# First loads on the sync engine's queue, and the first norm's statistics half a step later in a SwiGLU gate and up loop

## The chip, the cores and the metric

The kernel runs on one core of a Trainium2 chip. The core has five engines that run side by side, each through its own list of instructions in order: TensorE (PE in the profile; its weight loads are PEld), VectorE (DVE), ScalarE (ACT), GpSimd (POOL) and SyncE (SP). Data comes from HBM into SBUF by DMA; SP, ACT and POOL issue the transfers, and a transfer lands some microseconds after its issue. Products are summed in PSUM banks, of which the kernel keeps six in a pool called `sd` and two in a pool called `mm`.

The metric is the device time of one execution in microseconds. Before the change it is 1267.71 us, the median of three runs from 1267.32 to 1268.02.

## The reference, cut to what matters

Two layers, each of a SwiGLU block, a mixer (attention and gated linear attention) and another SwiGLU block, on 256 tokens of width 1024. The change touches only the very first SwiGLU block:

```python
def rmsnorm(x, g):
    xf = x.astype(jnp.float32)
    y = xf * lax.rsqrt(jnp.mean(xf * xf, axis=-1, keepdims=True) + EPS)
    return (y * g.astype(jnp.float32)).astype(x.dtype)

def swiglu(x, w_gate, w_up, w_down):
    return (jax.nn.silu(x @ w_gate) * (x @ w_up)) @ w_down

x = x + 0.5 * swiglu(rmsnorm(x, ffn1_norm[l]), ffn1_w_gate[l], ffn1_w_up[l], ffn1_w_down[l])
```

## The kernel before

The tokens lie transposed: eight blocks of 128 features by 256 tokens (`self.x`, tile `xs`). Every float32 operand is split into a high part in a reduced format and a low part, the rest: `split_x` (lines 158 to 164) multiplies a block by the norm's gain, makes the high part on ACT (L161) and the low part on DVE (L162). Weights come as chunks of up to 1 MB. `Weights.load` issues a chunk's transfer on SP into a tile `raw` (three of them), `cast` makes the high part `wh` of half a chunk on ACT (L76), and `prep` calls `cast` for the next half and then makes the low part `wl` of the half cast before it on DVE (L86). A product is two matmuls, `wh` against both parts of x (L129, 512 columns) and `wl` against the high part (L130, 256 columns).

`ffn` (line 237) runs 22 steps for gate and up. Chunk i holds the gate and the up weights of step i, each 128 columns wide: the first half of the chunk is the gate's, the second half is the up's. A step has 8 pairs of matmuls for the gate into one bank of `sd` (tile `ff`), and 8 for the up into a second. So step 3 cannot do its up before the second half of chunk 3 has its low part. The norm's factor for a token does not go into x: the matmuls run on x times the gain, and the results are multiplied by the factor (`rbc`) afterwards. Until `rbc` is there, finished banks wait.

For a finished step, `gate` adds the two halves of the gate's bank (a copy on ACT, L138, and an add on DVE, L139), multiplies by `rbc` (L248) and takes the Silu on ACT (L249); `gate2` multiplies by `rbc` (L253); `up` does L138 and L139 on the up's bank, multiplies the two (L260) and makes the high part on ACT (L261). The low part of the result (L265) is put off in the list `lows`.

`rbc` comes from a chain: squares of x on ACT (L1153), three adds on DVE (L1182 to L1185) that leave `acc`, a sum over the partitions on PE (`stat`, tile `st`), mean and eps on DVE (`rstd_col`, L192), the power −0.5 on POOL (L194), a broadcast over the partitions on PE (`rstd_row`, tile `rb`, L150) and a copy (L202) on DVE. In the first block (`start`) step 0 mixes gate and up and only waits; `stat` stands on PE after the gate of step 1, `rstd_row` after its up; then the gate and up of steps 0 and 1 are finished together.

The order on every engine is the order in which the code issues (a manual schedule). At the start, `go` loads x in four quarters on ACT's queue and chunk 0 in four quarters on SP's, then chunk 1 in three pieces, part of the constants, and chunk 2 in two; a small Silu on ACT brings in its table (L1114), and PE multiplies zeros (`wb`, L150) until data is there.

Of the kernel before, what the change touches and what calls it, by code (L numbers as in the profile page):

```python
# [17 lines left out]
T = 256  # L18
# [83 lines left out]
class Trunk:  # L102
# [75 lines left out]
        self._uid = getattr(self, "_uid", 0) + 1  # L178
        return self._uid

    def stat(self):
        self.st = self.bank(f"st{self.uid()}")
        self.sums(self.acc, True, True)

    def sums(self, sq, first, last):
# [7 lines left out]
        self.rs = self.small([P, 2], "rs")  # L193
        nc.gpsimd.tensor_tensor(self.rs, ms, self.mhalf[:, 0:2], op=OP.pow)  # L194

    def rstd_row(self):
        nc = self.nc
        b = self.bank(f"rb{self.uid()}")
        for tt in range(2):
            self.mm(b[:, tt * P : tt * P + P], self.rs[:, tt : tt + 1].to_broadcast([P, P]), self.ident)  # L200
        self.rbc = self.prb.tile([P, T], F32, name=f"rbc{self.uid()}", tag="rbc")
        nc.vector.tensor_copy(self.rbc, b[:, 0:T])  # L202
# [34 lines left out]
    def ffn(self, l, f, next_gain, hook=None):  # L237
        nc, W = self.nc, self.W
        start = l == 0 and f == 0
        hs = []  # L240
        lows = []

        def gate(i, b):

            u = self.t2(f"u{self.uid()}")
            g = u[:, 0:T]
            self.halves(g, b)
            nc.vector.tensor_mul(g, g, self.rbc)  # L248
            nc.scalar.activation(g, g, AF.Silu)  # L249
            return u  # L250

        def gate2(u):
            nc.vector.tensor_mul(u[:, 0:T], u[:, 0:T], self.rbc)  # L253

        def up(i, u, b):
            if i % 2 == 0:
                hs.extend(self.splits("h", 2))
            h = u[:, T : 2 * T]
            self.halves(h, b)
            nc.vector.tensor_mul(h, u[:, 0:T], h)  # L260
            nc.scalar.activation(hs[i][0], h, AF.Copy)  # L261
            lows.append((hs[i][1], h, hs[i][0].bitcast(F32)))

        def low():
            nc.vector.tensor_sub(*lows.pop(0))  # L265

        wait = None
        for i in range(NFF):
            wh, wl = W.take()
            bs = [self.bank(f"ff{self.uid()}") for _ in range(2)]  # L270
            if i == 0:
                for k in range(NK):
                    for n in range(2):
                        r = n * NK + k
                        self.mm2(bs[n], wh[:, r], wl[:, r], self.xx[k], k == 0, k == NK - 1)
                if not start:
                    self.stat()
                    self.rstd_col()
                    W.prep()
                W.prep()  # L280
                wait = bs
                continue
            for k in range(NK):
                self.mm2(bs[0], wh[:, k], wl[:, k], self.xx[k], k == 0, k == NK - 1)
            if i == 1:
                if start:
                    self.stat()
                    self.rstd_col()
                    self.constants()
                else:  # L290
                    self.rstd_row()
                    u0 = gate(0, wait[0])
                    gate2(u0)
                    up(0, u0, wait[1])
            if not (i == 1 and start):
                u = gate(i, bs[0])
            W.prep()
            if not (i == 1 and start):
                gate2(u)
            for k in range(NK):  # L300
                self.mm2(bs[1], wh[:, NK + k], wl[:, NK + k], self.xx[k], k == 0, k == NK - 1)
            if i == 1 and start:
                self.rstd_row()
                u0 = gate(0, wait[0])
                W.prep()
                gate2(u0)
                up(0, u0, wait[1])
                u = gate(i, bs[0])
                W.prep()
                gate2(u)  # L310
                up(i, u, bs[1])
            else:
                up(i, u, bs[1])
                W.prep()
            low()
            if hook:
                hook(i)
        while lows:
            low()
        for j in range(NK):  # L320
            b = self.bank(f"dn{self.uid()}", "mm")
            for half in range(2):
                wh, wl = W.take()
                for r in range(11):
                    k = half * 11 + r
                    self.mmx(j, b, wh[:, r], wl[:, r], hs[k], k == 0, k == NFF - 1)
                if half == 0 or j < NK - 1:
                    W.prep()
                    W.prep()
                if next_gain is None and half == 0 and j > 0:  # L330
                    self.final_x(j - 1)
                    if j == NK - 1:
                        self.st = self.bank("stl")
                        self.sums(self.acc, True, False)
            self.add_half(j, b)
            if next_gain is None:
                self.square(j, own=j == NK - 1)
                xg = self.t2(f"xg{j}")[:, 0:T]
                nc.vector.tensor_scalar(xg, self.x[j], self.final[:, j : j + 1], None, op0=OP.mult)
                self.xg[j] = xg  # L340
            else:
                self.post_x(j, next_gain[:, j : j + 1])
        W.prep()
        W.prep()
# [717 lines left out]
    def go(self):  # L1062
        from contextlib import ExitStack

        nc, tc, a = self.nc, self.tc, self.a
        with ExitStack() as st:
# [35 lines left out]
            sm = cp.tile([P, 80], F32, name="sm")  # L1102
            first = pools["raw"].tile([P, 2048], F32, name="raw0", tag="raw")
            view = lambda t, p: t.rearrange("p (n k c) -> p n k c", n=2, k=NK)[:, :, 2 * p : 2 * p + 2, :]

            for p in range(4):
                nc.scalar.dma_start(self.xs[:, 2 * p : 2 * p + 2, :], a["x"][:, 2 * p : 2 * p + 2, :])
                nc.sync.dma_start(view(first, p), view(a["gu"][0, 0, 0], p))
                if p == 0:
                    nc.scalar.dma_start(sm, a["sm"])  # L1110
            W.n_load = 1
            warm = self.small([P, 2], "warm", 1)
            nc.vector.memset(warm, 0.0)
            nc.scalar.activation(warm, warm, AF.Silu)  # L1114

            idle = self.t2("idle")
            nc.vector.memset(idle, 0.0)
            wb = self.bank("wb")
            for n in range(7):
                self.mm(wb[:, n % 2 * T : n % 2 * T + T], idle[:, 0:P], idle[:, 0:T])  # L1120
            gain = lambda l, n: sm[:, (l * 3 + n) * 8 : (l * 3 + n) * 8 + 8]
            self.final = sm[:, 48:56]
# [15 lines left out]
            nc.vector.memset(self.mhalf, -0.5)  # L1138
            w0 = W.split[0] = tuple(pools["w"].tile([P, 2048], F32R, name=f"w{x}0", tag=f"w{x}") for x in "hl")
            for p in range(4):  # L1140
                for j in (2 * p, 2 * p + 1):
                    self.split_x(j, gain(0, 0)[:, j : j + 1])
                nc.scalar.activation(view(w0[0], p), view(first, p), AF.Copy)  # L1143
                nc.vector.tensor_sub(view(w0[1], p), view(first, p), view(w0[0], p).bitcast(F32))  # L1144
            w1 = W.split[1] = tuple(pools["w"].tile([P, 2048], F32R, name=f"w{x}1", tag=f"w{x}") for x in "hl")
            for s in (slice(0, 512), slice(512, 1024)):
                nc.scalar.activation(w1[0][:, s], W.raw[1][:, s], AF.Copy)
                nc.vector.tensor_sub(w1[1][:, s], W.raw[1][:, s], w1[0][:, s].bitcast(F32))
            W.at, W.n_prep = (1, 1), (1, 0)
            W.load(1 + N_RAW)  # L1150
            sq = [self.t4(f"sq{x}") for x in range(2)]
            for x in range(2):
                nc.scalar.activation(sq[x].rearrange("p (j t) -> p j t", j=4), self.xs[:, 4 * x : 4 * x + 4, :], AF.Square)  # L1153
# [24 lines left out]
                    nc.gpsimd.memset(t, 0.0)  # L1178

            self.constants = constants  # L1180
            W.cast()
            nc.vector.tensor_add(sq[0], sq[0], sq[1])  # L1182
            nc.vector.tensor_add(sq[0][:, 0:512], sq[0][:, 0:512], sq[0][:, 512:1024])
            self.acc = self.psq.tile([P, T], F32, name="acc0", tag="acc")
            nc.vector.tensor_add(self.acc, sq[0][:, 0:256], sq[0][:, 256:512])  # L1185
            W.prep()

            def bias_hook(i):
                if i == 5:
# [34 lines left out]
            for tt in range(2):  # L1224
                for e in range(2):
                    o = self.t2(f"out{tt}{e}")
                    b = self.fin[tt][e]
# [92 lines left out]
```

## Time and profile before

| | |
|---|---|
| median of three runs | 1267.71 us |
| profiled execution | 1268.17 us |
| its span | 1266.4 us |
| PE busy | 1251.6 us, 99% |
| DVE busy | 913.9 us, 72% |
| ACT busy | 711.8 us, 56% |

The span runs from the first to the last instruction in the trace; the profiled execution is 1.77 us longer than its span. Times in the rows are counted from the span's start. PE's ends are modelled, so starts are the safer number there. Where a row merges several instructions (x2, x3), it gives the first start and the time to the last end.

### The profile page before, as it was taken

How to read it: one execution, taken by the hardware profiler on the slowest of the kernel's cores; microseconds unless marked ns; L12 is line 12 of the kernel's file. 1: busy time of each engine (PE TensorE's matmuls, PEld its weight loads, DVE VectorE, ACT ScalarE, POOL GpSimd, SP SyncE). 2: the span in 40 equal slices, each digit the busy share in tenths (PEclk: the TensorE clock that was granted, in tenths of full speed). 3: DMA queues.
4: the chain of work that ended last, by engine and by line, in shares of the span. 5: the costliest groups of instructions: out<-in, count | busy, mean ns of one | idle time of the engine just before them, and what ended most of it. 6: DMA issues, size and time to landing. Idle time of an engine off the chain costs nothing.

```text
span 1266.4 us, 18985 instructions
## 1 busy us (share of the span) xinstructions
PE 1251.6 (99%) x7396; PEld 1076.0 (85%) x7396; DVE 913.9 (72%) x1690; ACT 711.8 (56%) x1265; POOL 50.5 (4%) x60
## 2 busy tenths in 40 slices
PE   9999999999999999999999999999999999999997
PEld 7888889987778888888888888999777788888886
DVE  6888766774755778886578886567656668888753
ACT  5666545566644556655456664456675445566542
POOL 2001101000010000000010000010000100000000
PEclk9999999999999999999999999999999999999999
DMA  7576767334534445545665546573344354555451
GB/s 272 193 230 211 255 201 264 132 124 137 178 118 144 181 168 205 187 154 198 209 224 208 179 150 205 173 283 135 111 156 164 103 199 148 184 200 185 165 190 59
DMA packets 41001, 227.43 MB, mean 180 GB/s; under 512 B 6949, under 2 KB 8109, under 8 KB 21328
## 3 DMA queue, kind: packets, MB, share of 16 engines
q1 hardware_dynamic: 34352, 213.27, 48.7%
q0 software_dynamic: 5840, 11.87, 2.8%
q8 instruction: 58, 0.95, 0.3%
q10 hardware_dynamic: 720, 1.09, 0.3%
q14 instruction: 31, 0.25, 0.1%
HBM read 225.12 MB, written 2.63 MB: 180 GB/s over the span
## 4 chain that ended last, share of the span: by engine, by line
PE 80%; issue 15%; DVE 2%; ACT 2%; DMA 1%; POOL 0%; POOLq 0%; DVEq 0%; ACTq 0%
PE ff L129 19%; PE ff L130 10%; PE dn L129 9%; PE mm L122 7%; PE mm L123 6%; PE mm L124 6%; PE dn L130 4%; PE wo L129 2%; PE mg L122 2%; PE mg L124 2%; PE mg L123 2%; PE O L150 2%; PE o L150 1%; PE s L150 1%; PE wo L130 1%
## 5 line engine op out<-in xcount | busy, mean ns | idle before, releaser
L76 ACT ACTIVATE wh<-raw 128x1024 fp32r<-128x1024 f32 (+3 forms) x445 | 423.4, 967 | 183.6 <-issue 112.3
L86 DVE TENSOR_TENSOR wl<-raw,wh 128x1024 fp32r<-128x1024 f32 (+3 forms) x445 | 491.3, 1119 | 44.0 <-ACT wh L76 43.7
L129 PE MATMUL ff<-xs,wh 128*128 128x512 f32 x1408 | 489.9, 392 | 0.4 <-DVE xs L162 0.4
L130 PE MATMUL ff<-xs,wl 128*128 128x256 f32 x1408 | 393.9, 280 | 0.7 <-DVE wl L1144 0.5
L129 PEld LDWEIGHTS ff<-xs,wh 128*128 128x128 f32 x1408 | 264.4, 188 | 59.2 <-ACT wh L1143 0.8
L130 PEld LDWEIGHTS ff<-xs,wl 128*128 128x128 f32 x1408 | 264.3, 188 | 1.7 <-DVE wl L1144 1.1
L129 PE MATMUL dn<-h,wh 128*128 128x512 f32 x616 | 218.3, 399 | 0.0
L130 PE MATMUL dn<-h,wl 128*128 128x256 f32 x616 | 173.0, 281 | 0.0
L129 PEld LDWEIGHTS dn<-h,wh 128*128 128x128 f32 x616 | 115.7, 188 | 28.3
L139 DVE TENSOR_TENSOR u<-ff,u 128x256 f32<-128x256 f32 x176 | 74.7, 425 | 60.9 <-ACT u L138 60.9
L130 PEld LDWEIGHTS dn<-h,wl 128*128 128x128 f32 x616 | 116.4, 189 | 0.0
L122 PE MATMUL mm<-wh,xs 128*128 128x512 f32 x256 | 106.2, 415 | 2.5 <-DVE rt L541 2.5
L123 PE MATMUL mm<-wl,xs 128*128 128x512 f32 x256 | 101.5, 396 | 0.0
L124 PE MATMUL mm<-wh,xs 128*128 128x512 f32 x256 | 100.9, 394 | 0.0
L249 ACT ACTIVATE u<-u 128x256 f32<-128x256 f32 x88 | 36.8, 419 | 90.8 <-DVE u L248 90.8
L261 ACT ACTIVATE h<-u 128x256 fp32r<-128x256 f32 x88 | 36.8, 418 | 83.9 <-DVE u L260 83.9
L122 PE MATMUL mm<-xs,wh 128*128 128x256 f32 x256 | 73.8, 288 | 0.0
L124 PE MATMUL mm<-xs,wl 128*128 128x256 f32 x256 | 71.7, 280 | 0.0
L123 PE MATMUL mm<-xs,wh 128*128 128x256 f32 x256 | 71.6, 280 | 0.0
L138 ACT ACTIVATE u<-ff 128x256 f32<-128x256 f32 x176 | 65.6, 373 | 9.8 <-PE ff L130 5.4
L355 DVE SCALAR_TENSOR_TENSOR xs<-dn,xs 128x256 f32<-128x256 f32 x60 | 25.5, 424 | 56.0 <-PE dn L130 38.5
L122 PEld LDWEIGHTS mm<-wh,xs 128*128 128x128 f32 x256 | 48.1, 188 | 19.3 <-issue 4.7
(244 smaller groups left out, 1618.1 us busy)
## 6 DMA issues: line engine op xcount, KB each, us to landing
raw<-in_gu SPq DMA_DIRECT2D x85, 1024.0 KB, 4.9
raw<-in_wd SPq DMA_DIRECT2D x64, 704.0 KB, 4.1
raw<-in_wr SPq DMA_DIRECT2D x32, 1024.0 KB, 4.8
raw<-in_wt SPq DMA_DIRECT2D x16, 1024.0 KB, 5.1
raw<-in_wb SPq DMA_DIRECT2D x12, 1024.0 KB, 4.8
w<-in_w POOLq DMA_DIRECT2D x16, 512.0 KB, 8.6
raw<-in_wo SPq DMA_DIRECT2D x8, 1024.0 KB, 4.9
raw<-in_vg SPq DMA_DIRECT2D x4, 592.0 KB, 3.7
```

Source lines behind the costliest of these rows:

```text
L76: self.nc.scalar.activation(wh[:, s], self.raw[c][:, s], AF.Copy)
L86: self.nc.vector.tensor_sub(wl[:, s], self.raw[c][:, s], wh[:, s].bitcast(F32))
L122: mm(out, lh, rh, start=first, stop=False, skip_group_check=True)
L123: mm(out, lh, rl, start=False, stop=False, skip_group_check=True)
L124: mm(out, ll, rh, start=False, stop=last, skip_group_check=True)
L129: mm(b, lh, x[2], start=first, stop=False, skip_group_check=True)
L130: mm(b[:, 0:T], ll, x[0], start=False, stop=last, skip_group_check=True)
L138: self.nc.scalar.activation(o, b[:, T : 2 * T], AF.Copy)
L139: self.nc.vector.tensor_add(o, b[:, 0:T], o)
L150: self.nc.tensor.matmul(out, l, r, start=first, stop=last, skip_group_check=True)
L249: nc.scalar.activation(g, g, AF.Silu)
L261: nc.scalar.activation(hs[i][0], h, AF.Copy)
```

## The change

First loads: ACT issues only the first quarter of x and the small table of gains; SP issues the rest, quarters of x and of chunk 0 in turn. PE multiplies zeros five times in place of seven, on a tile cleared to half its width. In the first splits, a quarter of chunk 0 is cast between the two blocks of x that go with it.

Statistics: the second half of chunk 1 and the first half of chunk 2 are cast on ACT before the squares, and the low part of chunk 1's second half is made before the adds of the squares. `stat` moves behind the up of step 1, `rstd_row` behind the gate of step 2; both take their bank from the pool `mm`. Steps 0 and 1 are then finished after `rstd_row`, in the middle of step 2, one after the other with no `prep` between. The loops for the other three SwiGLU blocks come out in the order they had.

```diff
-    def stat(self):
-        self.st = self.bank(f"st{self.uid()}")
+    def stat(self, tag="sd"):
+        self.st = self.bank(f"st{self.uid()}", tag)
...
-    def rstd_row(self):
+    def rstd_row(self, tag="sd"):
         nc = self.nc
-        b = self.bank(f"rb{self.uid()}")
+        b = self.bank(f"rb{self.uid()}", tag)
...
             for k in range(NK):
                 self.mm2(bs[0], wh[:, k], wl[:, k], self.xx[k], k == 0, k == NK - 1)
-            if i == 1:
-                if start:
-                    self.stat()
-                    self.rstd_col()
-                    self.constants()
-                else:
-                    self.rstd_row()
-                    u0 = gate(0, wait[0])
-                    gate2(u0)
-                    up(0, u0, wait[1])
-            if not (i == 1 and start):
+            late = i < 2 and start
+            if i == 1 + start:
+                self.rstd_row("mm" if start else "sd")
+                for n, b in enumerate(wait):
+                    u = gate(n, b[0])
+                    gate2(u)
+                    up(n, u, b[1])
+            if not late:
                 u = gate(i, bs[0])
             W.prep()
-            if not (i == 1 and start):
+            if not late:
                 gate2(u)
             for k in range(NK):
                 self.mm2(bs[1], wh[:, NK + k], wl[:, NK + k], self.xx[k], k == 0, k == NK - 1)
-            if i == 1 and start:
-                self.rstd_row()
-                u0 = gate(0, wait[0])
-                W.prep()
-                gate2(u0)
-                up(0, u0, wait[1])
-                u = gate(i, bs[0])
-                W.prep()
-                gate2(u)
-                up(i, u, bs[1])
+            if late:
+                self.stat("mm")
+                self.rstd_col()
+                self.constants()
+                wait.append(bs)
             else:
                 up(i, u, bs[1])
-                W.prep()
-            low()
+            W.prep()
+            if late:
+                continue
+            while len(lows) > 1:
+                low()
...
-            for p in range(4):
-                nc.scalar.dma_start(self.xs[:, 2 * p : 2 * p + 2, :], a["x"][:, 2 * p : 2 * p + 2, :])
-                nc.sync.dma_start(view(first, p), view(a["gu"][0, 0, 0], p))
-                if p == 0:
-                    nc.scalar.dma_start(sm, a["sm"])
-            W.n_load = 1
             warm = self.small([P, 2], "warm", 1)
             nc.vector.memset(warm, 0.0)
+            nc.scalar.dma_start(self.xs[:, 0:2, :], a["x"][:, 0:2, :])
+            nc.scalar.dma_start(sm, a["sm"])
+            for p in range(4):
+                if p:
+                    nc.sync.dma_start(self.xs[:, 2 * p : 2 * p + 2, :], a["x"][:, 2 * p : 2 * p + 2, :])
+                nc.sync.dma_start(view(first, p), view(a["gu"][0, 0, 0], p))
+            W.n_load = 1
...
-            nc.vector.memset(idle, 0.0)
+            nc.vector.memset(idle[:, 0:T], 0.0)
             wb = self.bank("wb")
-            for n in range(7):
+            for n in range(5):
...
             for p in range(4):
-                for j in (2 * p, 2 * p + 1):
-                    self.split_x(j, gain(0, 0)[:, j : j + 1])
+                self.split_x(2 * p, gain(0, 0)[:, 2 * p : 2 * p + 1])
                 nc.scalar.activation(view(w0[0], p), view(first, p), AF.Copy)
                 nc.vector.tensor_sub(view(w0[1], p), view(first, p), view(w0[0], p).bitcast(F32))
+                self.split_x(2 * p + 1, gain(0, 0)[:, 2 * p + 1 : 2 * p + 2])
...
             W.load(1 + N_RAW)
+            W.cast()
+            W.prep()
             sq = [self.t4(f"sq{x}") for x in range(2)]
...
             self.constants = constants
-            W.cast()
             nc.vector.tensor_add(sq[0], sq[0], sq[1])
...
             nc.vector.tensor_add(self.acc, sq[0][:, 0:256], sq[0][:, 256:512])
-            W.prep()
```

Two places show what the change moves. The first is ACT around the squares `sq`. Before, with chunk 1 as `raw_123`, chunk 2 as `raw_128` and chunk 3 as `raw_167`:

```order
L1147 ACTIVATE wh_161<-raw_123 128x512 x2
L1153 ACTIVATE sq_169<-xs 128x1024
L1153 ACTIVATE sq_170<-xs 128x1024
L76 ACTIVATE wh_161<-raw_123 128x1024
L76 ACTIVATE wh_178<-raw_128 128x1024 x2
L76 ACTIVATE wh_269<-raw_167 128x1024
L138 ACTIVATE u_296<-ff_184 128x256
```

After the change, with chunk 1 as `raw_121`, chunk 2 as `raw_126` and chunk 3 as `raw_165`:

```order
L1143 ACTIVATE wh_159<-raw_121 128x512 x2
L76 ACTIVATE wh_159<-raw_121 128x1024
L76 ACTIVATE wh_168<-raw_126 128x1024
L1151 ACTIVATE sq_174<-xs 128x1024
L1151 ACTIVATE sq_175<-xs 128x1024
L76 ACTIVATE wh_168<-raw_126 128x1024
L76 ACTIVATE wh_236<-raw_165 128x1024 x2
L138 ACTIVATE u_314<-ff_182 128x256
```

The second half of chunk 1 and the first half of chunk 2 now stand ahead of the two squares. The second place is DVE from the copy of `rbc` to the low part of chunk 3's second half. Before, `u_296` is step 0 and `u_309` step 1:

```order
L202 COPY rbc_294<-rb_291 128x256
L139 TENSOR_TENSOR u_296<-ff_184,u_296 128x256
L248 TENSOR_TENSOR u_296<-u_296,rbc_294 128x256
L86 TENSOR_TENSOR wl_270<-raw_167,wh_269 128x1024
L253 TENSOR_TENSOR u_296<-u_296,rbc_294 128x256
L139 TENSOR_TENSOR u_296<-ff_185,u_296 128x256
L260 TENSOR_TENSOR u_296<-u_296 128x256
L139 TENSOR_TENSOR u_309<-ff_220,u_309 128x256
L248 TENSOR_TENSOR u_309<-u_309,rbc_294 128x256
L86 TENSOR_TENSOR wl_270<-raw_167,wh_269 128x1024
```

After the change `u_314` is step 0, `u_325` step 1 and `u_335` step 2; the copy of `rbc` and the first L139 of `u_314` stand just ahead of this piece, and the low part of chunk 3's first half stands ahead of the copy:

```order
L248 TENSOR_TENSOR u_314<-u_314,rbc_312 128x256
L253 TENSOR_TENSOR u_314<-u_314,rbc_312 128x256
L139 TENSOR_TENSOR u_314<-ff_183,u_314 128x256
L260 TENSOR_TENSOR u_314<-u_314 128x256
L139 TENSOR_TENSOR u_325<-ff_218,u_325 128x256
L248 TENSOR_TENSOR u_325<-u_325,rbc_312 128x256
L253 TENSOR_TENSOR u_325<-u_325,rbc_312 128x256
L139 TENSOR_TENSOR u_325<-ff_219,u_325 128x256
L260 TENSOR_TENSOR u_325<-u_325 128x256
L139 TENSOR_TENSOR u_335<-ff_291,u_335 128x256
L248 TENSOR_TENSOR u_335<-u_335,rbc_312 128x256
L86 TENSOR_TENSOR wl_237<-raw_165,wh_236 128x1024
```

The low part of chunk 3's second half stood behind one finished step and the start of a second; now it stands behind two finished steps and the start of a third.

## Rows read from the trace of the kernel before

**Rows 1.** The page's head: span, then each engine's busy time, share, count.

```profile
span 1266.4 us, 18985 instructions
PE 1251.6 (99%) x7396; PEld 1076.0 (85%) x7396; DVE 913.9 (72%) x1690; ACT 711.8 (56%) x1265; POOL 50.5 (4%) x60
```

**Rows 2.** Busy time by stretch: PE, PEld, DVE, ACT, POOL, clock, DMA share, GB/s.

```profile
10.00:15.00 5.00, 4.77 (x27) 3.86 (x27) 3.83 (x8) 4.34 (x8) 0.00 (x0) 1.00 1.02 391
...
30.00:200.00 170.00, 170.00 (x1004) 149.58 (x1003) 134.14 (x226) 97.88 (x172) 13.22 (x15) 1.00 0.65 212
...
1260.00:1262.00 2.00, 0.00 (x0) 0.00 (x0) 1.41 (x2) 1.26 (x2) 0.29 (x1) 1.00 0.06 22
...
1264.00:1266.00 2.00, 0.00 (x0) 0.00 (x0) 0.00 (x0) 0.00 (x0) 0.00 (x0) 0.50 0.35 128
```

**Rows 3.** Timeline of PE: start, duration, line, tile, idle before and its releaser.

```profile
7.59 0.49 PE L129 MATMUL ff<-xs,wh 128*128 128x512 f32 x1 [0.39 <-DVE xs L162]
...
18.88 0.38 PE L130 MATMUL ff<-xs,wl 128*128 128x256 f32 x1 [0.19 <-DVE wl L86]
...
21.77 0.71 PE L150 MATMUL rb<-cst,rs 128*128 128x128 f32 x4
...
27.88 0.39 PE L129 MATMUL ff<-xs,wh 128*128 128x512 f32 x1
...
30.88 0.28 PE L130 MATMUL ff<-xs,wl 128*128 128x256 f32 x1
```

**Rows 4.** Timeline of DVE from the squares' adds to chunk 3's second half.

```profile
15.28 1.23 DVE L1182 TENSOR_TENSOR sq<-sq,sq 128x1024 f32<-128x1024 f32 x1 [1.05 <-ACT sq L1153]
...
17.61 2.35 DVE L86 TENSOR_TENSOR wl<-raw,wh 128x1024 fp32r<-128x1024 f32 x2
...
22.86 0.41 DVE L139 TENSOR_TENSOR u<-ff,u 128x256 f32<-128x256 f32 x1
23.31 0.43 DVE L248 TENSOR_TENSOR u<-u,rbc 128x256 f32<-128x256 f32 x1
23.65 1.22 DVE L86 TENSOR_TENSOR wl<-raw,wh 128x1024 fp32r<-128x1024 f32 x1
24.79 0.42 DVE L253 TENSOR_TENSOR u<-u,rbc 128x256 f32<-128x256 f32 x1
...
27.08 0.42 DVE L139 TENSOR_TENSOR u<-ff,u 128x256 f32<-128x256 f32 x1 [0.76 <-ACT u L138]
...
27.88 1.22 DVE L86 TENSOR_TENSOR wl<-raw,wh 128x1024 fp32r<-128x1024 f32 x1
```

**Rows 5.** Timelines of ACT and, last row, POOL: splits, squares, casts, first Silu, power.

```profile
6.13 0.89 ACT L161 ACTIVATE xs<-xs,sm 128x256 fp32r<-128x256 f32 x2
...
7.47 0.91 ACT L161 ACTIVATE xs<-xs,sm 128x256 fp32r<-128x256 f32 x2
...
12.21 1.14 ACT L1147 ACTIVATE wh<-raw 128x512 fp32r<-128x512 f32 x2
13.26 1.99 ACT L1153 ACTIVATE sq<-xs 128x1024 f32<-128x1024 f32 x2
15.15 2.94 ACT L76 ACTIVATE wh<-raw 128x1024 fp32r<-128x1024 f32 x3
...
23.77 0.42 ACT L249 ACTIVATE u<-u 128x256 f32<-128x256 f32 x1 [2.46 <-DVE u L248]
...
20.11 1.60 POOL L194 TENSOR_TENSOR rs<-ms,mhalf 128x2 f32<-128x2 f32 x1 [19.66 <-DVE ms L192]
```

**Rows 6.** Issues: ACT's gains and SP's chunk 2, and their times to landing.

```profile
1.16 0.45 ACTq L1110 DMA_DIRECT2D sm<-in_sm  x1
...
8.77 0.88 SPq L56 DMA_DIRECT2D raw<-in_gu  x2
...
sm<-in_sm ACTq DMA_DIRECT2D x1, 40.0 KB, 4.1
...
raw<-in_gu SPq DMA_DIRECT2D x1, 512.0 KB, 6.2
```

More of the change, by code (lines that the diff above doesn't have):

```diff
@@ L280, in ffn @@
                 W.prep()
-                wait = bs
+                wait = [bs]
                 continue
```

## The prediction

> **What bounds the kernel now.** I read the page's head first: of a span of 1266.4 us PE is busy for 1251.6, or 99%, while DVE has 72% and ACT 56% [rows 1]. Then the stretches: from 30 to 200 us PE is busy for all of 170 us and the clock is at its upper level [rows 2]. So nothing that the change does can win time after 30 us; it can win only by bringing PE earlier to the point from which it runs without a break, or lose by breaking that run. A good mark for this is one matmul in step 3: the first L130 of its up half, the first that needs the low part of chunk 3's second half. Before, it starts at 30.88 [rows 3]. That low part, the last L86 of the DVE rows, starts at 27.88 and takes 1.22, so it is ready at 29.10, 1.78 us ahead [rows 4]. Whatever 30.88 becomes, the end moves by the same amount, as long as PE runs unbroken behind it.
>
> What sets the start is read from the chain for the norm's factor. Squares on ACT start at 13.26 [rows 5], the adds on DVE at 15.28, the two L86 behind them at 17.61 [rows 4], the power on POOL at 20.11 [rows 5], the broadcast `rb` on PE at 21.77 [rows 3], and the first L139 that finishes step 0 at 22.86 [rows 4]. Before, PE was held at few places by it and little. The question is whether that holds after the change.
>
> **The change part by part.** The first loads. ACT loses three issues, so its table comes in early; its first split then waits for the gains, issued at 1.16 and landed 4.1 us later, at 5.26 [rows 6], and not until 6.13 [rows 5]. That is 0.87 us won at the head. Two multiplications of zeros fewer, and the half cleared tile, cost and win nothing on the path: PE waited for x already, 0.39 us before 7.59 [rows 3].
>
> The order on ACT behind it decides what becomes of this. The cast of chunk 2's first half now stands ahead of the squares. Call its start L. It cannot start before that half has landed. Before, the half was issued at 8.77 and landed 6.2 us later, at 14.97 [rows 6]; it was cast only afterwards, so the landing held up nothing. The same bytes go ahead of it after the change (x, gains, chunk 0, chunk 1, some constants), and from 10 to 15 us the DMA engines are full, share 1.02 at 391 GB/s [rows 2]. SP issues it somewhat earlier, as it no longer waits behind the mixed quarters, but the engines are the limit. The lower bound for L is ACT's own work: from 5.26, four quarters of split and cast at 1.34 each (7.47 less 6.13), 1.05 for the two casts of chunk 1 (12.21 to 13.26) and one cast of half a chunk, 0.95 (two squares of the same size, 13.26 to 15.15) [rows 5]: 5.26 + 5.36 + 1.05 + 0.95 = 12.62. The upper bound: three quarters of x, 0.75 MB by the front's tiling, go on SP's queue ahead of it and nothing is given back on ACT's; at 391 GB/s that is 1.9 us, so 16.9. I take L = 14.8, close to the landing that a row shows, a little earlier for the earlier issue.
>
> The Trainium skill, DMA: Bandwidth & Descriptors, section "Issuing engines are not separate DMA queues", speaks to this: transfers started on ScalarE, SyncE or GpSimd run on the same 16 DMA engines and interleave, and issuing from several saves only sequencer time. The share of 1.02 above agrees [rows 2]. By it L stays near 14.97 and the sum below would be 3.4; if a queue of its own made a transfer faster, L could go down to ACT's bound.
>
> From L on, every hand-off has a row. Squares at L + 0.95. First add 2.02 later (13.26 to 15.28). Adds 2.33 (15.28 to 17.61). Then two L86 of 128x1024 and the mean, until POOL starts, 2.50 (17.61 to 20.11); after the change these two are both halves of chunk 2, the same size. Power to `rb` 1.66 (20.11 to 21.77). `rb` to the first L139 1.09 (21.77 to 22.86) [rows 3 to 5]. In sum the first L139 stands at L + 10.55, and `rb` at L + 9.46. The squares thus start at 15.75 in place of 13.26: the chain, though its place on PE is half a step on, is itself 2.5 us later.
>
> Now the wait that is added. Between that L139 and the low part of chunk 3's second half stand two finished steps and two instructions on DVE, where one finished step and two stood. A finished step took 4.22 (22.86 to 27.08), with an L86 in it that holds the queue for 1.14 (23.65 to 24.79). Without it, at least 4.22 − 1.14 = 3.08. But the L86 covered the Silu on ACT, which ran from 23.77 to 24.19; now L253 waits for it and starts some 0.04 after its end, at 24.23, so 0.56 earlier than 24.79 and no more: 3.66 [rows 4, 5]. I take 3.35, about the middle, since ACT also loses a cast that held up its next copy. Two steps are 6.70; then L139 to L86 0.80 (27.08 to 27.88), the L86 1.22, and 0.05 to PE (17.61 + 1.22 = 18.83, and L130 at 18.88) [rows 3, 4]. Together 8.77 behind the first L139, so the mark stands at L + 10.55 + 8.77 = L + 19.32.
>
> What is queued behind it on PE: everything. Before, 24 pairs lay between `rb` and the mark, 30.88 − 21.77 = 9.11 us; now it is 16, half a step of 2.77 less (27.88 to 30.88, without the 0.23 from L129 to L130) [rows 3]: 6.34, so PE by itself would be there at L + 15.80. It waits 3.5 us, whatever L is. That is the core of this forecast: the gate and up of steps 0 and 1 are put on DVE in one piece, ahead of a weight half that PE needs in the middle of that piece.
>
> The sum: L + 19.32 − 30.88 = L − 11.56. With L = 14.8 the change loses 3.2 us. The bounds of L give 1.1 (12.62) and 5.3 (16.9); those of the finished step move it by 0.6 either way.
>
> What costs nothing, and why. `stat` and `rb` in banks of `mm`: that pool is empty until the down projection. Step 3's banks are freed by the two L139 of step 0, before PE is there. POOL's loads of constants go later with the power, but so do their users, all behind step 5. `low` for steps 0 and 1 is put off behind an L86, and its result is used only after step 21. Chunk 4's first half follows the late L86 on DVE by one finished half step, and PE needs it 2.8 us later; I allow 0 to 0.3 us there. DVE is busy for 134.14 of 170 us afterwards [rows 2], so it catches up.
>
> The profiled execution took 1268.17 us, span 1266.4 and 1.77 around it; the median of the runs is 1267.71. Span 1269.6, execution 1271.4; on the median 1267.7 + 3.2 = 1270.9 us.
>
> **The rivals.** First, no change: the weights come early. If SP's single order brings chunk 2's first half as soon as ACT is ready for it, L = 12.62 and the loss is 1.1 us, 1268.8 us. It decides from L = 14.1 down, where the loss is 2.5 us or 0.2%, about what a measurement of this kernel can tell from no change. For it: the half is issued earlier, and x and chunk 0 no longer mix with chunk 1. Against it: the DMA share of 1.02 [rows 2]. Second, a gain: the low part is not what PE waits for, because DVE gets to it in time. Then the head's 0.87 and the short wait for chunk 1's low part, 0.19 before 18.88 [rows 3], are won, 1.1 us: 1266.6 us. It needs the mark at 29.8, so L at 10.5, while ACT's bound alone is 12.62; only an error in the DVE order would allow it. Third, more loss: the clock. After the last products the clock is still at 1.00, the upper level (2.4 GHz), from 1260 to 1262 with PE idle, and at 0.50 (1.2 GHz) from 1264 to 1266 [rows 2]. The wait of 3.5 us comes near such a pause, and PE has another a little earlier, at `st`, whose adds end only at L + 5.3 = 20.1. If the clock falls, half a step behind it (2.77 us) takes twice as long: 3.2 + 2.8 = 6.0 us, 1273.7 us. The Trainium skill, TensorE: Matmul & The Clock Gate, Part 1, says as much: the idle array goes to 1.2 GHz and comes back only after sustained work. Against it: the pause here is shorter than the one at the end.
>
> **How the numbers follow.** The forecast has 0.62, with a range of its own from 2.5 to 4.1 us (L from 14.1 to 15.7), 1270.2 to 1271.8. The early weights have 0.20, the clock 0.13, the gain 0.05. Predicted is 1270.9. The range that leaves out the gain and the worst of the clock's cases goes from 1268.8 to 1273.4. Slower by over 0.2% are the forecast and the clock, 0.75; within 0.2% the early weights and most of the gain's case, 0.22; faster by over 0.2%, where the gain would have to be larger than its price, 0.03.
>
> **What would show it.** Right: in the profile after, ACT's first split near 5.3; the squares near 15.8, just behind a cast that waited for a DMA; `rb` near 24.3; PE idle for some 3.5 us in step 3, released by DVE's L86, and the mark near 34.1; from there to the end the same time as before. Wrong: the squares before 15, or no such wait in step 3, or a granted clock below 1.00 after it.

## The result and the profile after

The changed kernel takes 1288.99 us, the median of four runs (1288.46 to 1289.94), against 1267.63 us (1267.32 to 1268.02) before: a ratio of 1.0168, 95% interval 1.0153 to 1.0184, or 21.4 us more. The forecast was 3.2 us more. The profiled execution's span is 1286.8 us, 20.4 us above the 1266.4 of before [rows 1].

The start went nearly as forecast. These are PE's rows of the changed kernel at the three places of [rows 3]: the sum `st`, the broadcast `rb`, and the mark, the first L130 of step 3's up.

```profile
21.05 0.61 PE L150 MATMUL st<-ones,acc 128*128 128x1 f32 x4 [1.12 <-DVE acc L1182]
...
25.07 0.71 PE L150 MATMUL rb<-cst,rs 128*128 128x128 f32 x4
...
34.91 0.58 PE L130 MATMUL ff<-xs,wl 128*128 128x256 f32 x1 [3.33 <-DVE wl L86]
```

PE waits 3.33 us for the low part of chunk 3's second half, and the mark stands at 34.91, 4.03 us behind the 30.88 of [rows 3]. What leads to it is seen on ACT (its line L1151 is the squares) and DVE:

```profile
5.26 0.51 ACT L161 ACTIVATE xs<-xs,sm 128x256 fp32r<-128x256 f32 x1 [2.12 <-DMA sm<-in_sm]
...
15.59 1.06 ACT L76 ACTIVATE wh<-raw 128x1024 fp32r<-128x1024 f32 x1 [0.38 <-DMA raw<-in_gu]
16.56 1.99 ACT L1151 ACTIVATE sq<-xs 128x1024 f32<-128x1024 f32 x2
```

```profile
26.16 0.41 DVE L139 TENSOR_TENSOR u<-ff,u 128x256 f32<-128x256 f32 x1
...
29.50 0.42 DVE L139 TENSOR_TENSOR u<-ff,u 128x256 f32<-128x256 f32 x1 [0.76 <-ACT u L138]
...
33.63 1.22 DVE L86 TENSOR_TENSOR wl<-raw,wh 128x1024 fp32r<-128x1024 f32 x1
```

The squares start behind a cast that waited for its transfer, a finished step takes 3.34 us, and the L86 comes behind two of them.

That is 4 of 20.4 us. The waits of PE over the whole run show that it was not the only place (engine, line, what it waited for: total us, times, longest). Before and after:

```profile
PE mm L122 <- DVE rt L541: 2.5, 2, 1.2
...
PE ff L130 <- DVE wl L86: 0.2, 1, 0.2
```

```profile
PE ff L130 <- DVE wl L86: 6.0, 3, 3.3
PE mm L124 <- DVE wl L86: 4.9, 2, 2.5
PE mm L122 <- DVE rt L536: 2.6, 2, 1.3
PE vg L123 <- DVE wl L86: 2.1, 2, 1.0
```

The third of the four was there before, with 2.5 us. The other three are all for L86, a weight's low part, and most of this waiting lies hundreds of microseconds behind the edited code. Where each stage's first matmul starts, in both traces, shows where the time comes in:

| stage begins | before, us | after, us | later by | added in the stage ahead |
|---|---|---|---|---|
| down 1 | 134.20 | 139.81 | 5.61 | 5.61 |
| mixer 1 | 196.52 | 202.13 | 5.61 | 0 |
| gate and up 2 | 448.28 | 459.32 | 11.04 | 5.43 |
| down 2 | 571.22 | 582.54 | 11.32 | 0.28 |
| gate and up 3 | 633.54 | 644.86 | 11.32 | 0 |
| down 3 | 756.48 | 772.40 | 15.92 | 4.60 |
| mixer 2 | 818.80 | 834.72 | 15.92 | 0 |
| gate and up 4 | 1070.57 | 1090.56 | 19.99 | 4.07 |
| down 4 | 1193.51 | 1213.79 | 20.28 | 0.29 |

Four steps make the loss: the start, the head of each mixer, and the head of the third gate and up loop. The 0.28 of the second gate and up loop come in at one pair as well: an L86 on DVE starts at 473.23, takes 1.22 us and so ends at 474.45, and PE's L130 for that half starts at 474.50, which is 0.40 us behind its L129, where the pairs before it have 0.23. At the first mixer the DVE rows of the kernel before read:

```profile
191.01 2.35 DVE L86 TENSOR_TENSOR wl<-raw,wh 128x1024 fp32r<-128x1024 f32 x2
```

Both halves of the mixer's first chunk (128x1024 each) have their low parts at 193.36, 3.2 us before the mixer begins at 196.52. In the changed kernel, DVE and PE in the same place:

```profile
196.61 1.95 DVE L86 TENSOR_TENSOR wl<-raw,wh 128x640 fp32r<-128x640 f32 x2
...
204.07 1.90 DVE L86 TENSOR_TENSOR wl<-raw,wh 128x1024 fp32r<-128x1024 f32 x2
```

```profile
205.34 0.56 PE L124 MATMUL mm<-xs,wl 128*128 128x256 f32 x1 [2.46 <-DVE wl L86]
```

A row is named by its first instruction: the pair at 196.61 is the last half of a down chunk (640 wide) and the first half of the mixer's; that chunk's second half opens the pair at 204.07, behind the last block of the down projection. DVE makes the same halves in the same places of the code, but each place makes the half before the one it made. The kernel has been half a chunk behind with its weights since step 1, where the change calls `prep` once less: before, step 0 called it once and step 1 three times, one of them between `gate` and `gate2` of step 0 and one between those of step 1; now step 0 calls it once and step 1 twice. From step 2 on both call it twice a step, so the half is never made up.

The idle stretches alone do not fill the four steps. The clock does part of the rest (columns as in [rows 2]):

```profile
32.00:34.00 2.00, 0.00 (x0) 0.00 (x0) 1.21 (x4) 0.94 (x3) 0.31 (x1) 1.00 0.10 25
34.00:36.00 2.00, 1.09 (x4) 1.00 (x5) 1.74 (x4) 1.39 (x3) 0.00 (x0) 0.68 0.20 37
36.00:38.00 2.00, 2.00 (x8) 1.71 (x8) 2.00 (x4) 1.64 (x3) 0.00 (x0) 0.50 0.82 295
38.00:40.00 2.00, 2.00 (x13) 1.75 (x12) 1.97 (x5) 1.06 (x2) 0.00 (x0) 0.96 0.46 193
...
206.00:208.00 2.00, 2.00 (x11) 2.00 (x11) 0.00 (x0) 0.00 (x0) 0.00 (x0) 0.50 0.78 209
...
650.00:652.00 2.00, 2.00 (x8) 1.71 (x7) 0.00 (x0) 0.12 (x1) 0.00 (x0) 0.50 0.92 385
...
838.00:840.00 2.00, 2.00 (x17) 2.00 (x18) 0.56 (x1) 0.54 (x1) 0.00 (x0) 1.00 0.46 86
```

The waits of PE ahead of the last two of these rows, in the third loop and in the second mixer:

```profile
648.07 0.39 PE L130 MATMUL ff<-xs,wl 128*128 128x256 f32 x1 [2.47 <-DVE wl L86]
...
837.93 0.39 PE L124 MATMUL mm<-xs,wl 128*128 128x256 f32 x1 [2.46 <-DVE wl L86]
```

Behind three of the four long waits the granted clock is 0.50 (1.2 GHz) for about two to four microseconds while PE is at work again. Behind the fourth, at the second mixer, it stays at 1.00, though the wait is as long as that of the first mixer. What the clock costs comes out of comparisons. At the start the mark is 4.03 us late and the stage 5.61, so 1.58 came behind the mark. The first mixer loses 5.43 and the second, with the same waits and the clock at 1.00, 4.07, so 1.36 in the first. The third loop loses 4.60; in the third experiment below it has the same wait with the clock at 1.00 and loses 3.01, so 1.59. Together that is some 4.5 of the 20.4 us. The other 16 or so are the 4.03 us up to the mark and the waits for the later low parts, with what PE loses as it takes up its work behind them.

### The profile page after: what moved, and what is told of

Its sections match the earlier page's. It is cut to its first block, busy times and chain, and to the rows that moved or that the text cites. A ratio compares the mean times of both kernels' runs of the same rounds, so it can differ in the third digit from the quotient of the medians.

```text
span 1286.8 us, 18982 instructions
## 1 busy us (share of the span) xinstructions
PE 1259.0 (98%) x7392; PEld 1080.4 (84%) x7392; DVE 912.4 (71%) x1690; ACT 709.4 (55%) x1265; POOL 49.7 (4%) x60
## 4 chain that ended last, share of the span: by engine, by line
PE 48%; issue 44%; DVE 3%; ACT 2%; POOL 1%; DMA 1%; SPq 0%; POOLq 0%; DVEq 0%; ACTq 0%
PE mm L122 7%; PE mm L124 6%; PE mm L123 6%; PE ff L129 6%; PE ff L130 3%; PE dn L129 3%; PE wo L129 2%; PE mg L122 2%; PE mg L124 2%; PE mg L123 2%; PE O L150 2%; PE dn L130 1%; PE o L150 1%; PE s L150 1%; DVE wl L86 1%
## 5 line engine op out<-in xcount | busy, mean ns | idle before, releaser
L86 DVE TENSOR_TENSOR wl<-raw,wh 128x1024 fp32r<-128x1024 f32 (+3 forms) x445 | 490.3, 1118 | 32.5 <-ACT wh L76 31.0
L129 PE MATMUL ff<-xs,wh 128*128 128x512 f32 x1408 | 494.6, 395 | 0.6 <-ACT wh L1138 0.6
L76 ACT ACTIVATE wh<-raw 128x1024 fp32r<-128x1024 f32 (+3 forms) x445 | 418.1, 965 | 63.6 <-PE dn L129 15.4
L130 PE MATMUL ff<-xs,wl 128*128 128x256 f32 x1408 | 396.6, 282 | 6.0 <-DVE wl L86 6.0
L129 PEld LDWEIGHTS ff<-xs,wh 128*128 128x128 f32 x1408 | 266.7, 189 | 60.4 <-ACT wh L1138 1.3
L130 PEld LDWEIGHTS ff<-xs,wl 128*128 128x128 f32 x1408 | 266.8, 190 | 8.3 <-DVE wl L86 7.9
L129 PE MATMUL dn<-h,wh 128*128 128x512 f32 x616 | 218.4, 399 | 0.0
L130 PE MATMUL dn<-h,wl 128*128 128x256 f32 x616 | 173.0, 281 | 0.0
L129 PEld LDWEIGHTS dn<-h,wh 128*128 128x128 f32 x616 | 115.7, 188 | 28.5
L139 DVE TENSOR_TENSOR u<-ff,u 128x256 f32<-128x256 f32 x176 | 74.6, 424 | 64.5 <-ACT u L138 64.5
L130 PEld LDWEIGHTS dn<-h,wl 128*128 128x128 f32 x616 | 116.4, 189 | 0.0
L161 ACT ACTIVATE xs<-xs,sm 128x256 fp32r<-128x256 f32 x48 | 24.1, 508 | 100.5 <-DVE xs L350 98.4
```

The costliest lines, as they stand in the source:

```text
L76: self.nc.scalar.activation(wh[:, s], self.raw[c][:, s], AF.Copy)
L86: self.nc.vector.tensor_sub(wl[:, s], self.raw[c][:, s], wh[:, s].bitcast(F32))
L129: mm(b, lh, x[2], start=first, stop=False, skip_group_check=True)
L130: mm(b[:, 0:T], ll, x[0], start=False, stop=last, skip_group_check=True)
L139: self.nc.vector.tensor_add(o, b[:, 0:T], o)
```

## The experiments

**One prep call back, at the end of step 1** (in the changed kernel). It makes the low part of chunk 3's second half ahead of the long DVE piece and gives the lead back for the rest.

```diff
             W.prep()
+            if i == 1 and start:
+                W.prep()
             if late:
                 continue
```

> The changed kernel with one more prep call at the end of step 1, as many as the kernel before had. Theory (the change calls prep once less in step 1, so every later weight half is made half a chunk later for the whole run, and PE waits where stages meet): the waits at 205, 645 and 835 us and the one of 3.33 us in step 3 go, together with the low clock behind them; what is left is a start later by some 2.4 us (rb at 25.07, half a step behind, in place of 21.77): 1270 us. Rival (the later statistics and the long DVE piece alone cost the time, and the later waits have another cause, such as banks or the order of transfers): only the start's 5.6 us go, 1283 us.

Measured: 1269.68 us (1268.34 to 1270.5, 11 runs) against 1267.6 of before, ratio 1.0014 (1.0006 to 1.0023). 19.3 of the 21.4 us are back. PE's waits for L86 over the whole run:

```profile
PE ff L130 <- DVE wl L86: 0.7, 2, 0.6
```

Those at the mixers and the third loop are gone, as the theory has it; the rival's 1283 is excluded. The down projection begins at 136.58, 2.4 us later than before, as expected, but in part by luck: in this run `st` waited 1.73 us for `acc`, and the clock fell there, which was no part of the expectation. The changed kernel's run, with 1.12 us of waiting, shows 1.00 in the same stretch. In this run:

```profile
22.00:24.00 2.00, 2.00 (x8) 1.70 (x9) 2.00 (x3) 1.01 (x2) 0.83 (x1) 0.57 0.00 0
24.00:26.00 2.00, 2.00 (x8) 1.71 (x8) 1.36 (x2) 0.00 (x0) 2.00 (x4) 0.58 0.95 262
```

**The same call, but only at the end of step 8.** The start keeps what the change does to it.

```diff
             while len(lows) > 1:
                 low()
+            if i == 8 and start:
+                W.prep()
             if hook:
```

> The changed kernel with one more prep call, but only at the end of step 8, after the start is over. Theory (missing prep): the start keeps its loss of 5.6 us (down projection begins at 139.8 us in place of 134.2), everything behind it is as in the kernel before: 1267.6 + 5.6 = 1273.2 us. Rival (the later waits have another cause): 1289 us, with the waits at 205, 645 and 835 us still there.

Measured: 1274.42 us (1272.83 to 1274.54, 4 runs), ratio 1.0049 (1.0035 to 1.0063). The wait of 3.3 us in step 3 is there, none at the mixers or the third loop. So one call, far from the edited lines, takes back 14.6 us, and the start costs 6.8 in this run, 1.2 more than expected. Its profile has the fall of the clock behind step 3's wait and another behind `st`, which had waited 1.2 us, and its down projection begins at 140.68, 0.87 us later than in the changed kernel's profile:

```profile
22.00:24.00 2.00, 2.00 (x8) 1.71 (x8) 2.00 (x3) 0.00 (x0) 1.04 (x1) 0.51 0.25 29
...
36.00:38.00 2.00, 2.00 (x8) 1.71 (x8) 1.76 (x3) 1.05 (x3) 0.00 (x0) 0.50 0.62 123
```

**The kernel before with one call less, at the end of step 8.**

```diff
             else:
                 up(i, u, bs[1])
-                W.prep()
+                if not (i == 8 and start):
+                    W.prep()
             low()
```

> The kernel before with one prep call left out, at the end of step 8, and nothing else. Theory (missing prep): the start is unchanged and the later stages lose what they lose in the changed kernel, 20.4 - 5.6 = 14.8 us: 1282.4 us, with PE waiting for L86 at the first mixer, the third SwiGLU block and the second mixer. Rival (other cause): within 1 us of 1267.6 us.

Measured: 1282.97 us (1282.51 to 1283.58, 4 runs), ratio 1.0121 (1.0105 to 1.0136): 15.4 us lost by one call, with nothing else of the change in it. Its waits answer to those of the changed kernel, all but that of step 3:

```profile
PE mm L124 <- DVE wl L86: 4.9, 2, 2.5
PE ff L130 <- DVE wl L86: 2.7, 2, 2.5
...
PE vg L123 <- DVE wl L86: 2.1, 2, 1.0
```

In its profile the clock falls behind the wait of the first mixer only. The third loop has the changed kernel's wait, without the fall, and takes from 640.10 to 766.05, 3.01 us longer than before in place of 4.60:

```profile
643.31 0.39 PE L130 MATMUL ff<-xs,wl 128*128 128x256 f32 x1 [2.47 <-DVE wl L86]
```

```profile
644.00:646.00 2.00, 2.00 (x14) 1.75 (x13) 0.39 (x1) 1.37 (x2) 0.00 (x0) 1.00 0.82 229
```

**Products that nobody reads in two of the waits** (in the changed kernel), to keep PE at work.

```diff
+                        if r == 0 and l == 1 and f == 0:
+                            fill = self.bank("fill", "mm")
+                            for q in range(6):
+                                self.mm2(fill, wh[:, q], wl[:, q], self.xx[0], True, True)
...
+            if i == 3 and start:
+                fill = self.bank("fill", "mm")
+                for k in range(NK):
+                    self.mm2(fill, wh[:, k], wl[:, k], self.xx[k], True, True)
             for k in range(NK):
                 self.mm2(bs[1], wh[:, NK + k], wl[:, NK + k], self.xx[k], k == 0, k == NK - 1)
```

> The changed kernel with products that nobody reads in two of its waits: 8 pairs of matmuls (2.8 us) in step 3's wait of 3.33 us and 6 pairs in the third SwiGLU block's wait of 2.5 us. Theory (part of the loss is the lower clock behind a wait, 1.6 us behind the first and 2.1 us behind the second): the granted clock stays at 1.00 there, down projection 1 begins near 138.2 us in place of 139.8, and the time falls to about 1285.3 us. Rival (the clock costs nothing beyond the wait, or the fill delays PE): 1289 us or more.

Measured: 1285.27 us (1284.66 to 1286.23, 4 runs), 3.7 us less than the changed kernel and close to the 1285.3 expected. The clock stays up where it was 0.50:

```profile
36.00:38.00 2.00, 2.00 (x13) 1.79 (x12) 1.97 (x4) 1.08 (x2) 0.00 (x0) 1.00 0.67 193
...
650.00:652.00 2.00, 2.00 (x14) 1.75 (x13) 0.00 (x0) 0.00 (x0) 0.00 (x0) 1.00 0.72 299
```

But the two shares do not come out as expected. In the profile, which is that of the slowest of the four runs (1286.23), the down projection begins at 138.94, 0.9 us earlier than in the changed kernel and not 1.6: `st` waited 1.6 us there, and the clock fell behind it (0.50 from 22 to 24 us). The third loop is 1.6 us shorter (644.02 to 769.98) and not 2.1, as the clock's share in it is 1.59. What makes the median 3.7 us shorter and not 2.5 this one profile does not show. The mean granted clock is 0.996 or 0.997 in each of the four runs and 0.993 or 0.994 in each of the changed kernel's, so all of them have less of the low clock. The third loop alone would not prove that the products did it, since it kept the clock without them in the run above.

**The first loads alone** (the kernel before with the change's first loads, its five products of zeros and its split order; statistics and calls as before).

```diff
+            nc.scalar.dma_start(self.xs[:, 0:2, :], a["x"][:, 0:2, :])
+            nc.scalar.dma_start(sm, a["sm"])
+            for p in range(4):
+                if p:
+                    nc.sync.dma_start(self.xs[:, 2 * p : 2 * p + 2, :], a["x"][:, 2 * p : 2 * p + 2, :])
+                nc.sync.dma_start(view(first, p), view(a["gu"][0, 0, 0], p))
...
-            for n in range(7):
+            for n in range(5):
```

> The kernel before with the change's first loads, five products of zeros and its order of the first splits; statistics and prep calls as before. Theory (the first loads bring the head forward, and the statistics' place and the missing prep call lose the time): 0.3 to 0.9 us faster than before, 1266.7 to 1267.3 us. Rival (the loads themselves are part of the loss, e.g. by fewer products before the first real one and a lower clock): 1268.5 us or more.

Measured: 1267.3 us (1266.7 to 1269.26, 11 runs), ratio 0.9997 (0.9988 to 1.0006). Inconclusive between a gain of 0.5 us and none; a loss of 1 us or more is excluded. PE begins at 6.56 in place of 7.59, and gives it back at `st`, where it waits 1.5 us for the squares' adds in place of 0.5. The profile is that of the slowest of the 11 runs (1269.26): the clock falls behind that wait, and the down projection begins at 135.37, 1.17 us later than before:

```profile
17.70 0.60 PE L150 MATMUL st<-ones,acc 128*128 128x1 f32 x4 [1.48 <-DVE acc L1186]
```

```profile
20.00:22.00 2.00, 2.00 (x8) 1.71 (x8) 1.12 (x1) 0.63 (x2) 1.93 (x2) 0.50 0.77 291
```

**Squares in ACT's waits, and the lead kept.** Built from the above: the squares use the time in which ACT waits for chunk 1, and the halves that the long DVE piece would hold up are made ahead of it.

```diff
-            W.prep()
+            if not (i == 2 and start):
+                W.prep()
             if not late:
                 gate2(u)
...
             W.prep()
+            if i == 1 and start:
+                W.prep()
+                W.prep()
             if late:
                 continue
...
+            square4(0)
             for s in (slice(0, 512), slice(512, 1024)):
...
+            square4(1)
             W.cast()
+            nc.vector.tensor_add(sq[0], sq[0], sq[1])
             W.prep()
...
```

> The changed kernel with the squares in ACT's two waits for chunk 1 (first before its first quarter, second before its second half), the first add ahead of chunk 1's last L86, and two more prep calls at the end of step 1 and one fewer in the middle of step 2, so that the weights are as far ahead as before. Theory (with the lead of the weights kept, the place of the statistics costs only what the squares' late start costs): acc some 2 us earlier than 20.6, rb near 23.2 and no wait for L86 in steps 3 and 4: step 4 begins near 32.0 us in place of 33.43, 1266.2 us. Rival (the long DVE piece behind rb costs time in any case): 1269 us or more, with a wait for L86 in step 4 or 5.

Measured: 1266.3 us (1265.56 to 1267.24, 11 runs) against 1267.77, ratio 0.9990 (0.9981 to 0.9998): 1.5 us faster than before, a small gain whose interval just leaves out no change. PE's rows at the start, in the profile of the fastest of these runs (1265.56):

```profile
18.88 0.50 PE L150 MATMUL st<-ones,acc 128*128 128x1 f32 x4
...
22.11 0.61 PE L150 MATMUL rb<-cst,rs 128*128 128x128 f32 x4
```

Neither has a wait in front of it, and there is none for L86 in the whole run. The down projection begins at 132.00 in place of 134.20. On DVE three L86 now stand between the mean and the copy of `rbc`, where the changed kernel had one and then an idle stretch of 1.36 us:

```profile
19.50 2.36 DVE L86 TENSOR_TENSOR wl<-raw,wh 128x1024 fp32r<-128x1024 f32 x2
22.16 1.23 DVE L86 TENSOR_TENSOR wl<-raw,wh 128x1024 fp32r<-128x1024 f32 x1 [0.30 <-ACT wh L76]
23.31 0.42 DVE L202 COPY rbc<-rb 128x256 f32<-128x256 f32 x1
```

So with the squares early and the weights' lead kept, the later place of the statistics on PE costs nothing. This run changes both at once; what the lead alone is worth is read from the first run, 19.3 of the 21.4 us.

## Why the prediction was wrong

**What held.** The direction, and the start by its steps. ACT's first split was forecast near 5.3 and came at 5.26. The chunk's first half landed 7.5 us after its issue at 8.03, later than the 14.8 taken for L, and its cast started at 15.59. From there the sum held to a few hundredths, with the measured L of 15.59: L + 9.46 = 25.05 for `rb` (25.07), a finished step of 3.35 (3.34), the mark at L + 19.32 = 34.91 (34.91), a wait of 3.5 us (3.33). The shorter queue on ACT's side thus gave no earlier landing.

**What was mis-sized.** L was 0.8 us later than taken, 15.59 against 14.8. The clock behind the wait was a rival with 0.13 and 2.8 us; it came true with 1.58 us there, and the sign that the forecast had named, a granted clock below 1.00 behind the wait, is in the rows. The forecast compared the pause with the one at the end of the run and thought it too short; waits of 3.33 and of 2.47 us were both followed by 0.50. The Trainium skill, TensorE: Matmul & The Clock Gate, Part 1, has the idle array at 1.2 GHz until it has worked for a while again; the 0.50 from 36 to 38 us, with PE busy for all of it, agrees. Whether a given wait lets the clock fall was not to be told from its length: a wait of 2.47 us in the third loop has the fall in the changed kernel and not in the kernel before with one call less.

**The step that failed.** "Whatever 30.88 becomes, the end moves by the same amount, as long as PE runs unbroken behind it", and at the end "from there to the end the same time as before". The condition was taken as met because DVE is busy for only 134 of 170 us afterwards, so it "catches up". But a busy share says nothing of the order: DVE makes a half when its place in the code comes, not when it has time. The front's sentence that the other loops "come out in the order they had" holds for the calls; which half a call makes had moved by one everywhere. The number of calls was in the diff: step 1 of the first block had three `W.prep()` on its path and has two. The forecast never counts the calls; it has the first effect of the lost one, the late low part of chunk 3's second half in step 3, by the order on DVE, and puts the whole price there. No rival had a loss behind the start; the largest, with the clock, stood at 1273.7 us. The chain from 26 to 35 us was the first of four such places.

Shown by the runs: one call put in at step 8 takes back 14.6 us with the start left as it is; one call taken out at step 8 of the kernel before costs 15.4 us; the clock's part in the profile is some 4.5 us in three of four places. In the changed kernel's profile 5.6 us of the loss belong to the start: 3.2 forecast, 0.8 for the later L, 1.6 of clock. The run with the call at step 8 puts 6.8 us there, with a second fall of the clock, behind `st`.

**Left open.** Why the clock falls behind one wait of 2.47 us and not behind another is not shown. Nor was the spread of some 2 us between runs of the kernels with a wait at `st` looked into; that the clock falls behind that wait in one profile and not in another is seen, how often is not.

## What to carry to other kernels

Where a routine called from many places keeps its own counter (the next half to load, to cast, to split), count its calls on every path of an edit, before and after: one call less is no local change, it moves the work of every later call. The margin to check is then not at the edit but at each place where a stage changes its pattern, and the trace of before shows it: how long before its first use each such half is ready (3.2 us at the first mixer here). An engine's idle share does not restore a lead that program order has lost.

## What the runs showed of the hardware

A wait of PE of about 2.5 us can cost nearly twice its length: 2.47 us of waiting in the third loop made 4.6 us where the clock was granted at 0.50 for the work behind it, and 3.0 us in the run where it stayed at 1.00. The same wait is not punished alike each time: at the first mixer 3.5 us of waits cost 5.43, with the clock at 0.50 behind them, at the second 4.07, with the clock at 1.00. Shorter waits can be followed by it too, 1.48 us at `st` in the run with the first loads alone. With pairs of products that nobody reads, 8 in one such wait and 6 in another, the mean granted clock was 0.996 or 0.997 in place of 0.993 or 0.994, and the median 3.7 us shorter.
